# FFN of a diffusion step: weight parts and additions regrouped at the start of the up columns, prompt taps moved behind the sample taps, the last tile's product in two column halves

## Chip, core and metric

One core of one Trainium2 chip. The metric is the device time of one execution in microseconds (us); the kernel before took 1524.4 us (median of 3 runs, 1524.12 to 1524.8).

## What is computed

One layer of a diffusion backbone: a mixer of gated linear attention, then a feed-forward block with a convolution, for 128 prompt tokens and 1024 sample tokens (a grid of 16 rows of 64) with 1024 features. The change lies in the feed-forward block and the final norm:

```python
def conv_ffn(h, w_up, conv_w, conv_b, w_down, grid):
    u = dw_conv(h @ w_up, conv_w, conv_b, grid)      # 3x3 on the grid; width 3 on the prompt
    gate, up = jnp.split(u, 2, axis=-1)
    return (jax.nn.silu(gate) * up) @ w_down
...
    x = x + gate2 * conv_ffn(h, w_ffn_up, ffn_conv, b_ffn_conv, w_ffn_down, grid)
...
y_prompt = rmsnorm(xp, final_norm)
y_sample = rmsnorm(xs, final_norm)
```

The hidden width is 2816, which is 22 columns of 128; w_up gives each column a gate half and an up half. Everything is float32.

## The kernel before

**Numbers in two parts.** Each float32 operand is split into a high part (ScalarE copies it into the multiplier's format: `wuh`, `t4h`) and a low part (the rest, by a subtraction in `split_lo`, line 69: `wul`, `t4l`), and each product is three matmuls: high by high, low by high, high by low. Low parts are made by VectorE (DVE) or GpSimd (POOL).

**Seven products for eight.** Each up column multiplies two halves of the tokens with a 2x2 arrangement of weight blocks (11, 12, 21, 22) by a Winograd form: seven products of sums of weight blocks (s1 to s4) and sums of tokens (t1 to t4). `up(c, p)` is product p of column c: twelve 128x512 matmuls (line 1772). F and S are the column's two accumulators in PSUM, of 1024 tokens each (gate half and up half); there are three such buffers, so a column's S takes the buffer of the F or S before it once the convolution has read it. ScalarE copies some partial products out (`cp`, `u2p`), and DVE adds them into F and S.

**The convolution.** `conv_rows` lets ScalarE write the bias and the middle tap and DVE add eight taps (line 1937) of about 960 columns; `conv_prompt` does bias (line 1950) and two short taps (line 1954) for the prompt. The Silu (line 2033), the product of the two halves on POOL (line 2035) and a DMA to memory (`scr_g`) follow.

**Order.** For column 0 the order on each engine is written out by hand: `run(engine, fn)` appends an operation behind the last one of that engine. From column 1 on the order is set at build time by a scheduler that estimates durations. Around the change: `first_sums` (line 1848) makes t4, the last token sum, on DVE and splits it (`t4h` on ACT, `t4l` on DVE); between the two halves it splits weight block s1 of column 1 (line 1859, its low part on DVE) and does two F additions (lines 1861 and 1862). Then ACT and POOL split the other pairs of column 1 (11/12, s2/s4, 21/22), by `second_pair`. Column 0's prompt taps stand among its F taps.

**Down products.** After the 22 columns eight products of 11 weight pairs with w_down follow (line 2244), four banks of 128 tokens by 512 features each. At this seam POOL makes low parts of the first pairs (`wul`, `wl`) beside the last columns' gate products. The last product ends with `first_tokens`: for each of its four token tiles an addition into y with the gate (lines 2203 and 2204), a square with its sum on ACT (line 2208), and `finish` (lines 2215 to 2223): two small DVE steps, a power of -1/2 on POOL, two scalings, and the DMA out.

Of the kernel before, what the change touches and what calls it, by code (L numbers as in the profile page):

```python
# [8 lines left out]
F32 = mybir.dt.float32  # L9
# [8 lines left out]
P = 128  # L18
# [31 lines left out]
def kernel(ctx: ExitStack, tc: tile.TileContext, ins, outs, stop=None):  # L50
# [1696 lines left out]
    def split_slots(c, names, eng, both=False):  # L1747
# [9 lines left out]
        first = nc.scalar.activation(hi, raw, AF.Copy)  # L1757
        last = split_lo(eng, lo, raw, hi)
        return (first, last) if both else last
# [84 lines left out]
    def second_pair(*names):  # L1844
        with tc.issue_after(ran["act"].ins):
            ran["act"], ran["pool"] = split_slots(1, names, nc.gpsimd, both=True)

    def first_sums():
# [10 lines left out]
        run("act", lambda: nc.scalar.activation(hi, raw, AF.Copy))  # L1859
# [155 lines left out]
    def prompt_columns(c):  # L2015
# [9 lines left out]
        conv_prompt(pp[:, 1 if up_first else 0, :], c, acc[c][0])  # L2025
        conv_prompt(pp[:, 0 if up_first else 1, :], 22 + c, acc[c][1])
# [17 lines left out]
    for c in range(NHID + 1):  # L2044
# [47 lines left out]
        if c == 0:  # L2092
            up(c, 3)
            up_prompt(c, 0)
        if c and n:
# [19 lines left out]
        if c == 0:  # L2115
            run("act", copy_pt)
            second_pair("11", "12")
            with tc.issue_after(ran["act"].ins):
# [19 lines left out]
        if c == 0:  # L2138
            second_weights()
        elif n:  # L2140
# [51 lines left out]
    def load_y(t):  # L2192
# [3 lines left out]
        sq[t] = smp.tile([P, 4], F32, name=f"sq{t}", tag=f"sq{t}")  # L2196
# [3 lines left out]
    def add_gated(t, half, src, op=ALU.add):  # L2200

        e = ep.tile([P, 512], F32, name="e", tag="e")
        nc.vector.tensor_tensor(e, src, gate2[0 if t == 8 else 1][:, HF[half]], op=ALU.mult)
        nc.vector.tensor_tensor(ys[t][:, HF[half]], ys[t][:, HF[half]], e, op=op)

    def square(t, half):
        junk = ep.tile([P, 512], BF16, name="junk2", tag="junk2")
        nc.scalar.activation(junk, ys[t][:, HF[half]], AF.Square, accum_out=sq[t][:, half : half + 1])

    def finish(t, first):  # L2210

        y, q = ys[t], sq[t]
        last = 1 - first
        nc.vector.tensor_scalar(q[:, 2:3], q[:, first : first + 1], 1.0 / D, EPS, op0=ALU.mult, op1=ALU.add)
        nc.vector.scalar_tensor_tensor(  # L2215
            q[:, 2:3], q[:, last : last + 1], 1.0 / D, q[:, 2:3], op0=ALU.mult, op1=ALU.add
        )
        nc.gpsimd.tensor_tensor(q[:, 3:4], q[:, 2:3], mhalf[:, 0:1], op=ALU.pow)  # L2218
        nc.scalar.activation(y[:, HF[first]], y[:, HF[first]], AF.Copy, scale=q[:, 3:4])
# [3 lines left out]
        nc.sync.dma_start(y_prompt[0] if t == 8 else y_sample[0, t * P : (t + 1) * P, :], y)  # L2223

# [7 lines left out]
    def product(banks, start, stop, done, tail=0, head=0, beside={}):  # L2232

        for js in ([tuple(range(head))] if head else []) + [(j,) for j in range(head, NPAIR - tail)] + ([tuple(range(NPAIR - tail, NPAIR))] if tail else []):
# [4 lines left out]
            for i in range(4):  # L2239
                ts_ = slice(i * P, (i + 1) * P)  # L2240
                for j, w in zip(js, ws):
                    for n, (a, b) in enumerate(((0, 0), (0, 1), (1, 0))):
                        with tc.issue_after(anchor["down"].ins) if j < head else nullcontext():
# [139 lines left out]
```

## Time and profile before

| what | us |
|---|---|
| median of 3 runs | 1524.4 |
| profiled execution, whole | 1526.4 |
| its span in the trace | 1524.6 |
| PE busy (12494 matmuls) | 1470.2 (96%) |
| DVE busy | 1146.5 (75%) |
| ACT busy | 779.9 (51%) |
| POOL busy | 707.7 (46%) |
| mean granted TensorE clock | 0.992 |

PE is TensorE, PEld its weight loads, DVE VectorE, ACT ScalarE, POOL GpSimd, SP SyncE (which issues DMAs). Times in the trace count from the start of the span. PE's share is an average: to see what one edit can do, one reads what PE waits for in that stretch, since a wait of another engine matters only where PE comes to wait for it in turn. In a row of the trace `t4l<-acc,t4h` is the tile written and the tiles read, and L69 the line of the program.

### The profile page before, as it was taken

What the parts mean: (1) busy time and instruction counts of PE and PEld (TensorE: products, weight loads), DVE (VectorE), ACT (ScalarE), POOL (GpSimd) and SP (SyncE); (2) the same over time, 40 slices, a digit from 0 to 9 for tenths busy, and PEclk for the clock granted to TensorE, in tenths of its full rate; (3) what the DMA queues carried; (4) which work ended last, traced back from release to release, by engine and by line L of the source; (5) the groups of instructions that cost most, each with busy time, mean ns of one, the idle gap of its engine ahead of it and who ended that gap; (6) DMA issues with size and microseconds to landing.
All of it is one profiled execution on the core that took longest, in us unless ns stands there. A gap on an engine that the chain in (4) does not pass through costs nothing.

```text
span 1524.6 us, 31105 instructions
## 1 busy us (share of the span) xinstructions
PE 1470.2 (96%) x12494; PEld 1250.5 (82%) x12494; DVE 1146.5 (75%) x1731; ACT 779.9 (51%) x1517; POOL 707.7 (46%) x538
## 2 busy tenths in 40 slices
PE   6999999999999999899989999999999999999997
PEld 2798989999898998777777888888888877888886
DVE  3766566664565767656689999999999999689475
ACT  3575667555454555513664444454444444466444
POOL 1512123234233241223237999999999995100001
PEclk9999999999999999999999999999999999999999
DMA  9311111335435463777642564545644567979752
GB/s 335 136 43 48 47 54 52 121 93 191 139 108 173 126 204 119 273 275 258 221 146 78 179 191 113 148 116 143 193 116 139 171 159 229 352 257 371 238 189 115
DMA packets 173802, 253.79 MB, mean 166 GB/s; under 512 B 11828, under 2 KB 113698, under 8 KB 171738
## 3 DMA queue, kind: packets, MB, share of 16 engines
q1 hardware_dynamic: 150455, 173.52, 35.5%
q0 software_dynamic: 22592, 77.60, 16.4%
q8 instruction: 98, 1.61, 0.5%
q10 hardware_dynamic: 611, 0.68, 0.1%
q14 instruction: 46, 0.38, 0.1%
HBM read 191.93 MB, written 82.90 MB: 180 GB/s over the span
## 4 chain that ended last, share of the span: by engine, by line
PE 81%; DVE 5%; DMA 5%; ACT 3%; issue 3%; POOL 2%; SPq 0%; POOLq 0%; ACTq 0%; DVEq 0%
PE u L1772 26%; PE mm L625 15%; PE xb L2244 7%; PE yb L2244 6%; PE mm L639 5%; PE x L2003 4%; PE mm L775 3%; PE lv L962 3%; PE yb L2296 2%; PE u L1542 2%; PE mm L519 1%; PE x L1030 1%; DVE acc L1937 1%; DMA mh<-scr_m 1%; DMA wa<-in_w_ada_dram 1%
## 5 line engine op out<-in xcount | busy, mean ns | idle before, releaser
L1937 DVE SCALAR_TENSOR_TENSOR acc<-u,convc,acc 128x945 f32<-128x945 f32 (+2 forms) x352 | 426.8, 1218 | 7.3 <-ACT acc L1925 0.2
L69 POOL TENSOR_TENSOR wl<-raw,wh 128x1024 fp32r<-128x1024 f32 x42 | 102.4, 2444 | 249.8 <-ACT wh L133 195.5
L625 PE MATMUL mm<-h1h,wh 128*128 128x384 f32 x528 | 185.0, 350 | 0.6 <-ACT qj L528 0.6
L625 PE MATMUL mm<-h1h,wl 128*128 128x384 f32 x528 | 179.0, 339 | 0.0
L625 PE MATMUL mm<-h1l,wh 128*128 128x384 f32 x528 | 179.0, 339 | 0.0
L925 DVE TENSOR_TENSOR Q<-Q,fb 128x384 f32<-128x384 f32 x126 | 83.8, 665 | 87.8 <-PE lv L962 86.9
L69 POOL TENSOR_TENSOR wul<-sr,wuh 128x512 fp32r<-128x512 f32 (+1 forms) x64 | 119.6, 1868 | 16.5 <-ACT wuh L1757 16.4
L69 POOL TENSOR_TENSOR wul<-ra,wuh 128x1024 fp32r<-128x1024 f32 x44 | 115.2, 2617 | 19.1 <-ACT wuh L1757 19.1
L915 ACT ACTIVATE m<-k 128x384 f32<-128x384 f32 x126 | 70.2, 557 | 81.9 <-PE lv L962 39.4
L2218 POOL TENSOR_TENSOR sq<-sq,mhalf 128x1 f32<-128x1 f32 x9 | 11.1, 1232 | 205.1 <-DVE sq L2215 205.1
L625 PEld LDWEIGHTS mm<-h1h,wh 128*128 128x128 f32 x528 | 99.5, 188 | 5.5 <-issue 3.9
L625 PEld LDWEIGHTS mm<-h1l,wh 128*128 128x128 f32 x528 | 99.5, 188 | 0.6 <-issue 0.2
L625 PEld LDWEIGHTS mm<-h1h,wl 128*128 128x128 f32 x528 | 99.3, 188 | 0.8 <-issue 0.5
L639 PE MATMUL mm<-wh,h1h 128*128 128x256 f32 x288 | 84.5, 293 | 0.6 <-ACT v L664 0.5
L927 DVE TENSOR_TENSOR k<-k,fb 128x384 f32<-128x384 f32 x126 | 74.2, 589 | 10.7 <-ACT m L915 6.2
L639 PE MATMUL mm<-wh,h1l 128*128 128x256 f32 x288 | 81.2, 282 | 0.0
L639 PE MATMUL mm<-wl,h1h 128*128 128x256 f32 x288 | 81.2, 282 | 0.0
L133 ACT ACTIVATE wh<-raw 128x1024 fp32r<-128x1024 f32 x50 | 52.8, 1058 | 42.2 <-PE mm L625 11.4
L2035 POOL TENSOR_TENSOR acc<-acc,acc 128x1152 f32<-128x1152 f32 x22 | 61.1, 2779 | 15.1 <-DVE acc L1937 15.1
L1965 ACT ACTIVATE u2p<-u 128x512 f32<-128x512 f32 x44 | 26.5, 602 | 77.8 <-PE u L1772 77.8
L1757 ACT ACTIVATE wuh<-ra 128x1024 fp32r<-128x1024 f32 x42 | 44.3, 1054 | 34.5 <-issue 18.4
L639 PEld LDWEIGHTS mm<-wh,h1h 128*128 128x128 f32 x288 | 55.1, 191 | 3.4 <-issue 1.7
(386 smaller groups left out, 4470.0 us busy)
## 6 DMA issues: line engine op xcount, KB each, us to landing
ra<-in_w_ffn_up_dram SPq DMA_DIRECT2D x84, 256.0 KB, 3.3
raw<-in_w_in_dram SPq DMA_DIRECT2D x32, 512.0 KB, 4.7
v<-in_w_ada_dram SPq DMA_DIRECT2D x27, 512.0 KB, 4.7
scr_g<-acc POOLq DMA_DIRECT2D x22, 576.0 KB, 5.7
scr_s<-late POOLq DMA_DIRECT2D x11, 1024.0 KB, 5.4
scr_t<-in_w_ffn_down_dram POOLq DMA_DIRECT2D x16, 704.0 KB, 7.3
wa<-in_w_ada_dram SPq DMA_DIRECT2D x16, 512.0 KB, 5.7
scr_t<-in_w_ffn_down_dram POOLq DMA_DIRECT2D x2, 2816.0 KB, 12.7
```

The lines of the kernel that those rows point to most:

```text
L69: return eng.tensor_tensor(out, full, hi.bitcast(F32), op=ALU.subtract)
L133: nc.scalar.activation(hi, raw, AF.Copy)
L625: anchor["fill"] = mm(ps, a[:, kt, :], h[kt][b], start=(n == 0), stop=(n == 23))
L639: anchor["fill"] = mm(ps, h[kt][t // 3][:, ts_], a[:, kt % 4, :], start=(n == 0), stop=(n == 23))
L915: nc.scalar.activation(aps(t, 0, [[2 * h, NB], [h, 2], [1, h]]), aps(src, 0, [[2 * h, NB], [BL + h, 2], [1, h]]), AF.Copy)
L925: nc.vector.tensor_tensor(qm, qm, aps(ff_, 2 * h - 1, [[BL - h, 2], [2 * h, NB], [0, h]]), op=ALU.mult)
L927: nc.vector.tensor_tensor(km, km, aps(ff_, BL + 2 * h - 1, [[-(BL + h), 2], [2 * h, NB], [0, h]]), op=ALU.mult)
L1772: last = mm(dst, w_slot(c, a, x)[:, kt, :], HB[y][b][:, kt, :], start=(start and n == 0), stop=(stop and n == 11), skip_group_check=True,)
L1937: last = nc.vector.scalar_tensor_tensor(o, u3[:, r0 + dy : r1 + dy, c0 + dx : c1 + dx], wc(3 * (dy + 1) + dx + 1), o, op0=ALU.mult, op1=AL ...
L2003: last = mm(pk, HB[h]["p"][:, 4 * half + kt, :], aps(flat(W[x]), a * 512 + kt * P, [[(b - a) * 512, 2], [1, P]]), start=(half + kt + n == ...
L2035: last = nc.gpsimd.tensor_tensor(accg, accg, accu, op=ALU.mult)
L2244: anchor["down"] = mm(banks[i], w[a][:, ts_], w[b][:, 512:1024], start=(start and j == 0 and n == 0), stop=(j == NPAIR - 1 and n == 2), sk ...
```

## The change

Three regroupings:

1. Weight block s1 of column 1 is split earlier: its high part on ACT ahead of t4h, its low part on DVE ahead of the token sums. The high part of 11/12 follows s1's on ACT, and its low part moves from POOL to DVE, behind the F additions. The t4 split on DVE goes ahead of the two F additions. `second_pair` becomes `second_hi` and `second_lo`; the pairs s2/s4 and 21/22 are split at the head of column 1's turn in the loop.
2. For columns 0 and 1 the prompt's bias and taps are issued behind the F taps (`after("conv")`).
3. In the last product the last bank is multiplied in two halves of 256 columns, all five tail pairs for the one half and then for the other; its addition and its square go by halves too, with one more small sum, and tile 2's last scaling and DMA go behind the second half's addition.

```diff
+    def second_hi(*names):
+        hi, second[names] = split_parts(1, names)
+        run("act", hi)
+    def second_lo(*names, eng="pool"):
+        run(eng, lambda: second[names](nc.vector if eng == "dve" else nc.gpsimd))
...
         half_hi("t4", 0, tmp[2])
-        slot = SLOT[1]["s1"]
-        hi, lo = (flat(W[x][:, slot]) for x in "hl")
-        raw = flat(at(1, "s1"))
-        run("act", lambda: nc.scalar.activation(hi, raw, AF.Copy))
-        run("dve", lambda: split_lo(nc.vector, lo, raw, hi))
-        run("dve", lambda: tt(F[:, 0:512], F[:, 0:512], copies["p1"], op=ALU.add))
-        run("dve", lambda: tt(F[:, 512:NS], F[:, 512:NS], copies["u2"], op=ALU.add))
         half_hi("t4", 1, tmp[3])
         for n in range(2):
             half_lo("t4", n, tmp[2 + n])
+        run("dve", lambda: tt(F[:, 0:512], F[:, 0:512], copies["p1"], op=ALU.add))
+        run("dve", lambda: tt(F[:, 512:NS], F[:, 512:NS], copies["u2"], op=ALU.add))
+        second_lo("11", "12", eng="dve")
...
-        conv_prompt(pp[:, 1 if up_first else 0, :], c, acc[c][0])
-        conv_prompt(pp[:, 0 if up_first else 1, :], 22 + c, acc[c][1])
+        with after("conv") if c < 2 else nullcontext():
+            conv_prompt(pp[:, 1 if up_first else 0, :], c, acc[c][0])
+            conv_prompt(pp[:, 0 if up_first else 1, :], 22 + c, acc[c][1])
...
+        if c == 1:
+            for names in (("s2", "s4"), ("21", "22")):
+                second_hi(*names)
+                second_lo(*names)
+            second_weights()
...
         if c == 0:
             up(c, 3)
             up_prompt(c, 0)
+            second_hi("s1")
+            second_lo("s1", eng="dve")
+            second_hi("11", "12")
...
-            second_pair("11", "12")
-            with tc.issue_after(ran["act"].ins):
+            with tc.issue_after(ran["act"].ins), tc.issue_after(ran["dve"].ins):
                 anchor["conv"] = conv_rows(F, c, acc[c][0])
             ran["act"] = anchor["rows"]
-            second_pair("s2", "s4")
-            second_pair("21", "22")
...
+                cols = pieces if last and i == 3 and js[-1] == NPAIR - 1 else (slice(0, 512),)
+                for cs in cols:
+                    for j, w in zip(js, ws):
...
+                                    banks[i][:, cs],
+                                    w[a][:, ts_],
+                                    w[b][:, 512 + cs.start : 512 + cs.stop],
...
+                    if len(cols) > 1:
+                        last(i, cs)
...
+    def last_piece(i, cs):
+        fs = slice(512 + cs.start, 512 + cs.stop)
+        added = add_gated(i, 1, yb[i][:, cs], cs=fs)
+        square(i, 1, cs=fs, to=1 if cs.start == 0 else 4)
+        if cs.start:
+            with tc.issue_after(added.ins):
+                finish_rest(i - 1, 0)
+            finish_root(i, 0, parts=(1, 4))
+            finish_rest(i, 0)
```

`finish` is cut into `finish_root` (the small sums, the power, and the scaling on ACT) and `finish_rest` (the scaling on DVE and the DMA).

What this does to the order on an engine is seen at three places. The first is DVE around the t4 split, before; 9783 and 10298 are the two halves of the token sum, cp and u2p the copies that the F additions (L1861, L1862) read, and 9782 is the tile of F's convolution.

```order
L1407 TENSOR_TENSOR acc_10298<-rb_9794,acc_10298 128x1024
L1854 TENSOR_TENSOR u<-u,u2p_10302 128x512
L69 TENSOR_TENSOR wul<-sr,wuh 128x512
L1861 TENSOR_TENSOR u<-u,cp_10251 128x512
L1862 TENSOR_TENSOR u<-u,u2p_10302 128x512
L69 TENSOR_TENSOR t4l<-acc_9783,t4h 128x4x256
L69 TENSOR_TENSOR t4l<-acc_10298,t4h 128x4x256
L1937 SCALAR_TENSOR_TENSOR acc_9782<-u,convc,acc_9782 128x15x63
```

And the same stretch of DVE after the change (L1867 and L1868 are the F additions, L1941 is a tap).

```order
L69 TENSOR_TENSOR wul<-sr,wuh 128x512
L1407 TENSOR_TENSOR acc_9783<-rb_9794,acc_9783 128x1024
L1407 TENSOR_TENSOR acc_10298<-rb_9794,acc_10298 128x1024
L1862 TENSOR_TENSOR u<-u,u2p_10302 128x512
L69 TENSOR_TENSOR t4l<-acc_9783,t4h 128x4x256
L69 TENSOR_TENSOR t4l<-acc_10298,t4h 128x4x256
L1867 TENSOR_TENSOR u<-u,cp_10251 128x512
L1868 TENSOR_TENSOR u<-u,u2p_10302 128x512
L69 TENSOR_TENSOR wul<-ra,wuh 128x2x512
L1941 SCALAR_TENSOR_TENSOR acc_9782<-u,convc,acc_9782 128x15x63
```

The s1 low part went ahead of the sums, t4l ahead of the two F additions, and the 11/12 low part (`wul<-ra`) came over from POOL.

The second place is POOL at the seam from the columns to the down products, before: L2035 is column 20's gate product (acc3), `scr_g20` its DMA, and `wul` and `wl` are low parts of the first down pairs.

```order
L2035 TENSOR_TENSOR acc3_10298<-acc3_10298,acc2_9783 128x1152
L1910 DMA scr_t3_157<-in_w_ffn_down_dram 32x11x512
L69 TENSOR_TENSOR wul_10293<-ra_10290,wuh_10292 128x1024
L69 TENSOR_TENSOR wul_10293<-sr_10291,wuh_10292 128x1024
L2036 DMA scr_g20_139<-acc3_10298 128x1152
L1892 TENSOR_TENSOR late_10471<-acc3_10298 128x512
L69 TENSOR_TENSOR wl0_14091<-raw0_14096,wh0_14090 128x1024
L69 TENSOR_TENSOR wl1_14093<-raw1_14097,wh1_14092 128x1024
L69 TENSOR_TENSOR wul_10293<-sr_10291,wuh_10292 128x1024
```

POOL at the same place after the change.

```order
L69 TENSOR_TENSOR wul_10293<-ra_10290,wuh_10292 128x1024
L2040 TENSOR_TENSOR acc3_10298<-acc3_10298,acc2_9783 128x1152
L1914 DMA scr_t3_157<-in_w_ffn_down_dram 32x11x512
L69 TENSOR_TENSOR wul_10293<-sr_10291,wuh_10292 128x1024
L69 TENSOR_TENSOR wl0_14091<-raw0_14096,wh0_14090 128x1024
L69 TENSOR_TENSOR wl1_14093<-raw1_14097,wh1_14092 128x1024
L2041 DMA scr_g20_139<-acc3_10298 128x1152
L1896 TENSOR_TENSOR late_10473<-acc3_10298 128x512
L69 TENSOR_TENSOR wul_10293<-sr_10291,wuh_10292 128x1024
```

The first low part (`wul<-ra`) now stands ahead of the gate product, and the two `wl` ahead of its DMA and of the token difference `late`.

The third place is PE in the last bank after the change, where the first column half ends and the second begins (wuh and wul, wh2 and wl2 are parts of the tail pairs; a wait is in brackets).

```order
L2264 MATMUL yb_15203<-wh2_14094,wl2_14095 128x256
L2264 MATMUL yb_15203<-wuh_10292 128x256
L2264 MATMUL yb_15203<-wul_10293,wuh_10292 128x256
L2264 MATMUL yb_15203<-wuh_10292,wul_10293 128x256
L2264 MATMUL yb_15203<-wuh_10292 128x256 [waits DVE_49]
```

Before, the bank had 15 matmuls of 128x512 and no wait; now it has 30 of 128x256, and the sixteenth waits for DVE, which reads the first half of the same bank.

More of the change, by code (lines that the diff above doesn't have):

```diff
@@ L1756, in split_slots @@
             raw = raw.rearrange("p (s n) -> p s n", s=2)
-        first = nc.scalar.activation(hi, raw, AF.Copy)
-        last = split_lo(eng, lo, raw, hi)
-        return (first, last) if both else last
+        return lambda: nc.scalar.activation(hi, raw, AF.Copy), lambda eng: split_lo(eng, lo, raw, hi)
+    def split_slots(c, names, eng):
+        hi, lo = split_parts(c, names)
+        hi()
+        return lo(eng)
     def weight_sums(c, eng):
@@ L2223, in finish @@
         nc.sync.dma_start(y_prompt[0] if t == 8 else y_sample[0, t * P : (t + 1) * P, :], y)
+    def finish(t, first):
+        finish_root(t, first)
+        finish_rest(t, first)
     def times_norm(t, half):
@@ L2230, in load_norm, with product @@
             nc.sync.dma_start(fn, ins["final_norm"].rearrange("(o d) -> o d", o=1).to_broadcast([P, D]))
-    def product(banks, start, stop, done, tail=0, head=0, beside={}):
+    def product(banks, start, stop, done, tail=0, head=0, beside={}, last=None):
         for js in ([tuple(range(head))] if head else []) + [(j,) for j in range(head, NPAIR - tail)] + ([tuple(range(NPAIR - tail, NPAIR))] if tail else []):
@@ L2319, in first_tokens @@
         square(i, 1)
-        finish(i, 0)
-    product(yb, False, True, first_tokens, tail=5)
+        finish_root(i, 0)
+        if i < 2:
+            finish_rest(i, 0)
[7 more added lines that the diff above has]
+            finish_root(i, 0, parts=(1, 4))
+            finish_rest(i, 0)
+    product(yb, False, True, first_tokens, tail=5, last=last_piece)
 _INS = [
```

64 lines of the change are left out of this document (30 added, 34 removed).

## The prediction

> **What bounds the kernel now.** I read the waits of PE first, from the first up column to the end.
>
> ```profile
> PE u L1772 <- DVE acc L1937: 3.4, 2, 2.6
> PE u L1772 <- DVE t4l L69: 2.7, 1, 2.7
> PE u L1772 <- ACT wuh L1859: 1.0, 1, 1.0
> PE xb L2244 <- POOL wul L69: 0.9, 1, 0.9
> PE u L1772 <- ACT cp L1965: 0.8, 1, 0.8
> ```
>
> After the columns are total us, count, longest. Some 9 us in 744 are all that PE loses to others here; everything else it works. The windows say the same, and show what a wait drags behind it (per stretch: length, PE, PEld, DVE, ACT, POOL busy, granted clock, DMA share, GB/s).
>
> ```profile
> 795.00:800.00 5.00, 5.00 (x16) 3.94 (x16) 4.87 (x6) 1.18 (x2) 5.00 (x3) 0.66 0.16 47
> 800.00:820.00 20.00, 17.79 (x88) 14.22 (x87) 17.60 (x18) 9.90 (x14) 11.75 (x9) 1.00 0.14 40
> 820.00:1250.00 430.00, 430.00 (x2105) 356.10 (x2104) 417.95 (x442) 200.01 (x268) 418.09 (x277) 1.00 0.53 150
> ...
> 1255.00:1260.00 5.00, 2.99 (x7) 2.42 (x8) 4.93 (x6) 1.17 (x1) 4.02 (x4) 0.69 0.97 308
> ```
>
> From 820 to 1250 PE is busy 430.00 of 430.00 us at full clock, so nothing that the change shuffles inside those columns can pay, and what is gained or lost before 820 is carried on unchanged. In the first and last row the clock falls to 0.66 and 0.69, each at a long wait. The chain of waits (start, length, what) gives the steps.
>
> ```profile
> 790.31 4.44 DVE t4l L69 x2
> ...
> 794.79 9.85 PE u L1772 x35
> 804.64 2.84 PE x L2003 x24
> ...
> 1285.14 21.83 PE xb L2244 x95
> 1306.97 29.92 PE yb L2244 x132
> ```
>
> A 128x512 product steps by 29.92/132 = 0.227 us, a 128x256 one by 2.84/24 = 0.118. Behind 1285.14 each piece of PE begins where the last one ends (1285.14 + 21.83 = 1306.97, and so on to the last product), so a delay there reaches the end whole. Three places can therefore move the time: the start of the columns (787 to 820), the seam to the down products (1267 to 1285), and the tail behind the last product.
>
> **First part, the start of the columns.** Two kinds of work are drawn forward and one is taken away.
>
> ```profile
> 780.67 2.35 DVE L69 TENSOR_TENSOR t3l<-acc,t3h 128x1024 fp32r<-128x1024 f32 x2
> ...
> 786.66 1.06 ACT L1410 ACTIVATE t4h<-acc 128x1024 fp32r<-128x1024 f32 x1 [5.38 <-DVE acc L1407]
> ...
> 788.27 0.69 DVE L69 TENSOR_TENSOR wul<-sr,wuh 128x512 fp32r<-128x512 f32 x1 [1.03 <-ACT wuh L1859]
> ...
> 790.21 4.52 DVE L69 TENSOR_TENSOR t4l<-acc,t4h 128x1024 fp32r<-128x1024 f32 x2
> 794.66 2.44 DVE L1937 SCALAR_TENSOR_TENSOR acc<-u,convc,acc 128x945 f32<-128x945 f32 x2
> ...
> 790.48 3.17 POOL L69 TENSOR_TENSOR wul<-ra,wuh 128x1024 fp32r<-128x1024 f32 x1 [19.11 <-ACT wuh L1757]
> ```
>
> Rows here and below are of the timeline: start, length, engine, line, and in brackets the idle time ahead and what ended it. ACT is idle 5.38 us ahead of t4h, and there the s1 hi part now goes: PE's 1.00 us wait disappears, and the s1 lo part (0.69, of which DVE steps 0.61) stands ahead of the token sums, which end near 787.2 instead of 786.6. Then the two t4l follow at once, with POOL not working: 2.35 as t3l's pair takes, not 4.52 beside POOL's 3.17. They end at 790.7; PE, 1.2 us earlier, waits some 0.5 for them instead of 2.7. The two F additions (0.69 each) and the 11/12 lo part, now DVE's (half of 2.35), come behind: F0's taps start at 793.3, 1.35 ahead of 794.66.
>
> Now what is late next. With no prompt taps among them the eight F0 taps (2.44/2 = 1.22 each, a little more where one needs the last) end near 803.3. S0's eight taps, four short prompt taps (0.3 each, an estimate: with 127 columns each is less than half an addition of 512) and three additions (0.69) are 13 us of DVE, with its short waits for the copies: 816.5. PE meanwhile is done with its independent work, which in the chain ends at 804.64 + 2.84 = 807.5, some 5.5 us earlier (waits of 1.0 and 2.2, and 1.7 of the slow clock behind 795), stands from 802 to 803.4 for F0's buffer (gap 1.5), ends up(1,1) at 806.2, and waits for the cp copy. That copy stands on ACT behind the Silu with its table load:
>
> ```profile
> 807.97 1.28 ACT L2033 ACT_TABLE_LOAD   x1
> 809.26 1.17 ACT L2033 ACTIVATE acc<-acc 128x1152 f32<-128x1152 f32 x1
> 810.34 0.58 ACT L1965 ACTIVATE cp<-u 128x512 f32<-128x512 f32 x1
> ...
> 818.46 0.47 PE L1772 MATMUL u<-t1h,wuh 128*128 128x512 f32 x1 [0.77 <-DVE acc L1937]
> ```
>
> The Silu needs the prompt taps, last at 804.8 now; 1.28, 1.17 and 0.58 from 805.3 give 808.1, a gap of 2.0 on PE instead of 0.8. Then 12 products, the u2 copy, 12 more to 814.5, and a wait for S0's last tap: the first product of column 2 starts at 816.6 instead of 818.46, **1.85 us earlier**, out of the 4 us that PE is ahead at 795. The rest has become three gaps of 1.5, 2.0 and 2.1.
>
> Gaps have a price. The windows at 0.66 and 0.69 hold the waits of 2.7 and 2.6; at 0.66, 0.34 of 5.00 us are missing, 1.7 us, which is 3.4 us at half clock, and PE pays it wherever it works through the whole of it. The Trainium skill ("TensorE: Matmul & The Clock Gate", Part 1: The HAM clock gate) has the half rate return only after an idle window of some 3.4 us; by that rule none of the new gaps costs anything, and the start is worth the full 1.85. This trace disagrees: 2.6 and 2.7 were enough.
>
> Waits of 0.8 drew none: the clock from 800 to 820, where the cp wait lies, is 1.00. Between 1.0 and 2.6 I have no row in these parts; 2.0 and 2.1 are nearer to 2.6, so I take a slow stretch after both. The first lengthens up(1,6) and by it the copy, S0's taps and the start of column 2 by 1.2; the second costs about 1.0, as PE stands through part of it. Term: -1.85 + 1.2 + 1.0 = **+0.35 us**; ends -1.85 (no stretch) and +1.5 (both paid in full, or one behind the 1.5 gap as well).
>
> **Second part, the seam.** Nobody edits it, but POOL's order there changes: pair 2's lo part (wul<-ra) now stands ahead of column 20's gate product.
>
> ```profile
> 1267.62 2.69 POOL L2035 TENSOR_TENSOR acc<-acc,acc 128x1152 f32<-128x1152 f32 x1 [7.46 <-DVE acc L1937]
> 1270.26 1.10 POOL L1910 DMA_DIRECT2D scr_t<-in_w_ffn_down_dram  x1
> 1270.98 2.83 POOL L69 TENSOR_TENSOR wul<-ra,wuh 128x1024 fp32r<-128x1024 f32 x1
> 1273.64 2.53 POOL L69 TENSOR_TENSOR wul<-sr,wuh 128x1024 fp32r<-128x1024 f32 x1
> 1275.98 0.73 POOL L2036 DMA_DIRECT2D scr_g<-acc  x1
> 1276.61 1.42 POOL L1892 TENSOR_TENSOR late<-acc 128x512 f32<-128x512 f32 x1
> 1277.87 4.86 POOL L69 TENSOR_TENSOR wl<-raw,wh 128x1024 fp32r<-128x1024 f32 x2
> 1282.60 2.49 POOL L69 TENSOR_TENSOR wul<-sr,wuh 128x1024 fp32r<-128x1024 f32 x1
> ...
> 1268.50 1.05 ACT L133 ACTIVATE wuh<-ra 128x1024 fp32r<-128x1024 f32 x1
> ...
> 1268.63 2.75 DVE L69 TENSOR_TENSOR wl<-ra,wh 128x1024 fp32r<-128x1024 f32 x1 [0.25 <-ACT wh L133]
> ...
> 1275.32 0.48 PE L2244 MATMUL xb<-wuh 128*128 128x512 f32 x1
> ```
>
> POOL has no idle time from 1267.62 to 1285.09, where pair 4's lo part releases PE. All eight instructions remain, in another order, so the end shifts as the start does. The queue's head now waits for ACT's hi part (1268.50 + 1.05 = 1269.55), and then beside DVE's wl (itself behind one more addition and S20's last tap, so near 1269.4 to 1270.6, at 1.2 without the product beside it). Two such operations at once took 2.75 and 2.83 instead of 1.2 and 2.4, one held up by the other; so POOL's first gets going at 1270.65, 3.03 later than 1267.62, and takes 0.26 less than its old step of 2.66. Pair 4 comes at 1285.09 + 3.03 - 0.26 = 1287.9, **+2.75 us**. On the way pair 3's lo part (needed by the eighth product from 1275.32, at 1277.0) comes at 1278.85, a gap of 1.9; pair 4's is then another of 2.0. A slow stretch after the first is hidden in the second. Ends: +1.7 where POOL starts at 1269.6 unhindered, +4.4 where the second gap draws a stretch of 1.7.
>
> **Third part, the tail.**
>
> ```profile
> 1516.02 0.39 PE L2244 MATMUL yb<-wuh,wul 128*128 128x512 f32 x1
> ...
> 1516.45 0.69 DVE L2203 TENSOR_TENSOR e<-yb,gate 128x512 f32<-128x512 f32 x1 [0.44 <-PE yb L2244]
> ...
> 1518.49 0.63 ACT L2208 ACTIVATE junk<-y 128x512 bf16<-128x512 f32 x1 [1.10 <-DVE y L2204]
> ...
> 1519.49 0.55 POOL L2218 TENSOR_TENSOR sq<-sq,mhalf 128x1 f32<-128x1 f32 x1 [2.85 <-DVE sq L2215]
> ...
> 1520.07 0.75 DVE L2220 SCALAR_TENSOR_TENSOR y<-y,sq,fn 128x512 f32<-128x512 f32 x1 [0.67 <-POOL sq L2218]
> ```
>
> From the last product's end (1516.41) to the last scaling's (1520.82) lie 4.41 us, with tile 2's scaling between the two additions. The second column half needs a multiplication and an addition of 128x256 (0.43 each, an estimate: 0.69 at 512 and 1.18 at 1024 give it by a straight line), a square (between 0.3 and 0.63; I take 0.4, and 0.2 until its sum is there, since 1518.49 + 0.63 is 0.4 ahead of the POOL row), then 0.16, 0.55 and 0.75 and hand-overs of 0.03 to 0.09: 3.2, so 1.2 less. Against it: 30 products of 0.118 are 0.14 longer than 15 of 0.227, and PE's first product of the second half waits for DVE's multiplication of the first (they share a bank): a product's end 0.3 after its start (0.39 at 512), the multiplication 0.43 behind tile 2's addition, hand-overs, together 0.75 beyond a step. Term: -1.2 + 0.14 + 0.75 = **-0.3 us**; ends -1.2 (wait gone) and +0.2 (128x256 as dear as 512).
>
> **Sum.** +0.35 + 2.75 - 0.3 = +2.8 us. Against the profiled execution's 1526.4 that is 1529.2; that execution lay 2.0 above the median of the runs, so for the median 1524.4 + 2.8 = **1527.2**. It is 0.18%, and 0.2% (3.05 us, about what a measurement of this kernel can tell from no change) is just not reached.
>
> **Rivals.**
> 1. Slower: half clock behind pair 4's gap. If the 1.9 gap for pair 3 draws no stretch and the 2.0 gap does, 1.7 is added whole, PE having no wait behind it. For it speaks 0.69 after 2.6; against it that the first gap is just as long. It decides from a gap somewhere between 1.0 and 2.6. 1527.2 + 1.7 = 1528.9.
> 2. No stretch after gaps of about 2 at the columns' start: 1524.4 - 1.85 + 2.75 - 0.3 = 1525.0. For it: the page's rule, and no row of a 2.0 gap there. Against: two of two long ones did.
> 3. The seam's order is harmless, POOL's chain having slack that the rows hide: 1524.4 + 0.35 - 0.3 = 1524.4 or, with rival 2, 1522.2. Against it stands that POOL has no idle time there and PE's one wait ends on it.
> 4. All goes well: rivals 2 and 3, PE's 0.9 wait gone too and the tail's wait absent: -1.85 - 0.9 - 1.2 = -3.95, 1520.4.
>
> **How the numbers follow.** Forecast 0.42; rivals 0.26, 0.15, 0.10, 0.07. The forecast's own spread (0.8 either way from where the slow stretches fall) puts 0.10 of its 0.42 beyond 3.05. Slower: 0.26 + 0.10 = 0.36; same: 0.32 + 0.15 + 0.10 = 0.57; faster: 0.07. The range leaves out rival 4, the deep end of 3, and the cases with more than one extra stretch: 1522.6 to 1529.6.
>
> **What would show it.** Right: t4l as two of 1.2 us and no PE wait for the s1 part; PE waits near 803, 806 and 814 of 1.6, 2.0 and 2.1 us, with a clock well below 1.00 behind them; two waits on POOL's wul of about 1.9 instead of one of 0.9; one PE wait on DVE's e of about 0.8 in the last bank. Wrong: one wait or none on POOL at the seam, or a clock of 1.00 from 806 to 825; then the sum is 2 to 3 us too high. Columns 2 to 19 with PE waits would break the step on which everything is carried.

## The result, and the profile after

The changed kernel takes 1527.47 us (median) against 1524.12 for the kernel before in the same runs: ratio **1.0031 [1.002, 1.0041]**, 0.31% or some 4.7 us slower, more than the 0.2% that a measurement can tell. By the two medians alone it is 3.35 us, 0.22%. One of its eleven runs took 2064 us at a granted clock of 0.65, and the ratio leaves it out. The profiled execution took 1530.77 us, with a span of 1528.8.

The waits of PE from the first up column to the end, after (total us, count, longest):

```profile
PE u L1775 <- DVE acc L1941: 3.8, 2, 2.6
PE xb L2264 <- POOL wul L69: 3.5, 2, 1.9
PE u L1775 <- ACT cp L1969: 2.1, 1, 2.1
PE u L1775 <- ACT wuh L1757: 2.0, 1, 2.0
PE u L1775 <- ACT u2p L1969: 0.7, 1, 0.7
PE yb L2264 <- DVE e L2213: 0.6, 1, 0.6
```

Against before, the wait for s1's high part (1.0) is gone and the one for t4l is down from 2.7 to 0.3. New or longer are the cp wait (0.8 before), a 2.0 us wait ahead of column 2, a second wait for POOL's low parts, and the one in the tail. The windows (length, PE, PEld, DVE, ACT, POOL busy, granted clock, DMA share, GB/s):

```profile
805.00:810.00 5.00, 2.94 (x11) 2.09 (x10) 4.26 (x6) 3.19 (x4) 3.92 (x4) 0.89 0.00 0
810.00:815.00 5.00, 4.31 (x14) 3.13 (x13) 2.85 (x4) 2.09 (x4) 0.90 (x1) 0.77 0.01 3
815.00:820.00 5.00, 3.02 (x12) 2.15 (x12) 4.91 (x6) 3.48 (x4) 5.00 (x3) 0.91 0.18 52
820.00:825.00 5.00, 5.00 (x19) 3.97 (x18) 4.86 (x5) 0.95 (x2) 5.00 (x4) 0.74 0.44 129
830.00:1250.00 420.00, 419.87 (x2059) 348.02 (x2058) 405.94 (x428) 195.69 (x262) 405.07 (x269) 1.00 0.53 150
```

From 800 to 820 the clock had been 1.00 before; now two half-clock stretches lie behind two waits of 2 us (0.89 with 0.77, and 0.91 with 0.74). From 830 to 1250 PE works 419.87 of 420.00 us, so what is lost ahead of it is carried to the end. Column start, after, PE's rows with a wait (start, length, ..., idle time ahead and what ended it):

```profile
803.20 0.50 PE L1775 MATMUL u<-b11h,wuh 128*128 128x512 f32 x1 [1.13 <-DVE acc L1941]
808.27 0.50 PE L1775 MATMUL u<-t2h,wuh 128*128 128x512 f32 x1 [2.06 <-ACT cp L1969]
813.56 0.50 PE L1775 MATMUL u<-t3h,wuh 128*128 128x512 f32 x1 [0.69 <-ACT u2p L1969]
818.56 0.47 PE L1775 MATMUL u<-t1h,wuh 128*128 128x512 f32 x1 [1.99 <-ACT wuh L1757]
```

The last row names a copy on ACT. In the program that product waits for this copy and for DVE's last S0 tap. The copy had long been made; what ended just ahead of the product is the tap, the first of the nine in the last row of DVE here:

```profile
788.07 2.36 DVE L69 TENSOR_TENSOR t4l<-acc,t4h 128x1024 fp32r<-128x1024 f32 x2 [0.52 <-ACT t4h L1410]
...
807.18 0.34 DVE L1958 SCALAR_TENSOR_TENSOR acc<-x,convc,acc 128x127 f32<-128x127 f32 x1
808.25 0.70 DVE L2119 TENSOR_TENSOR u<-u,cp 128x512 f32<-128x512 f32 x1 [0.73 <-ACT cp L1969]
...
813.54 0.70 DVE L2120 TENSOR_TENSOR u<-u,u2p 128x512 f32<-128x512 f32 x1 [2.12 <-ACT u2p L1969]
...
816.61 0.70 DVE L2145 TENSOR_TENSOR u<-u,u2p 128x512 f32<-128x512 f32 x1
817.22 11.13 DVE L1941 SCALAR_TENSOR_TENSOR acc<-u,convc,acc 128x945 f32<-128x945 f32 x9
```

The two t4l take 1.2 us each, as forecast. Later DVE stands idle for 2.12 us, waiting for a copy of what PE computes at half clock, and takes an S addition (L2145) ahead of that last tap. At ACT one sees why the cp copy is late:

```profile
804.80 0.46 ACT L1954 ACTIVATE acc<-x,vcol,convc 128x128 f32<-128x128 f32 x1 [2.25 <-DVE acc L1958]
805.28 1.28 ACT L2038 ACT_TABLE_LOAD   x1
806.57 1.16 ACT L2038 ACTIVATE acc<-acc 128x1152 f32<-128x1152 f32 x1
807.64 0.58 ACT L1969 ACTIVATE cp<-u 128x512 f32<-128x512 f32 x1
```

The prompt's bias on ACT waits 2.25 us for a prompt tap on DVE; table load, Silu and cp copy stand behind it in ACT's queue.

The seam, after: DVE's order, then POOL's.

```profile
1269.35 0.70 DVE L2120 TENSOR_TENSOR u<-u,u2p 128x512 f32<-128x512 f32 x1 [0.23 <-ACT u2p L1969]
1269.96 1.19 DVE L1941 SCALAR_TENSOR_TENSOR acc<-u,convc,acc 128x945 f32<-128x945 f32 x1
```

```profile
1271.30 3.26 POOL L69 TENSOR_TENSOR wul<-ra,wuh 128x1024 fp32r<-128x1024 f32 x1 [9.56 <-ACT wuh L133]
1274.52 2.70 POOL L2040 TENSOR_TENSOR acc<-acc,acc 128x1152 f32<-128x1152 f32 x1
...
1286.78 2.77 POOL L69 TENSOR_TENSOR wul<-sr,wuh 128x1024 fp32r<-128x1024 f32 x1
```

POOL starts its chain at 1271.30 instead of 1267.62, and ends it at 1289.55 instead of 1285.09; PE waits for its low parts 1.86 and 1.67 us where it had waited 0.89. On DVE column 20's last tap now stands behind column 21's second F addition. The tail:

```profile
1519.85 0.39 PE L2264 MATMUL yb<-wuh 128*128 128x256 f32 x1 [0.59 <-DVE e L2213]
```

**Where the time went.** To compare executions I count from the first product of column 0 with token sum t3 (at 782.26 before, 782.03 after), and put places in the program beside each other:

| us from there | before | after | difference | predicted |
|---|---|---|---|---|
| first product of column 2 | 36.20 | 36.53 | +0.33 | |
| first product of column 3 | 58.69 | 60.40 | +1.71 | |
| first down product | 493.06 | 494.96 | +1.90 | +0.35 |
| seam, to the second down product | 31.49 | 34.28 | +2.79 | +2.75 |
| from there to PE's end | 209.60 | 210.63 | +1.03 | +0.9 |
| PE's end to the last scaling | 4.41 | 3.13 | -1.28 | -1.2 |
| sum | 738.56 | 743.00 | +4.44 | +2.8 |

Seam and tail came as reckoned; the column start cost 1.55 us more in this execution. That row differs from one execution to the next: e1_seam, e7_dveseam and e10_both below leave the column start as it is in the kernel after. With the same two waits on PE (2.06 to 2.08 and 1.98 to 1.99), column 3 starts there at 58.92, 57.31 and 60.48, with one, no and two half-clock stretches. Why the seam moved at all was open.

### The profile page after: what moved, and what is told of

It is laid out like the page before. It is cut to its first block, busy times and chain, and to the rows that moved or that the text cites. A ratio compares the mean times of both kernels' runs of the same rounds, so it can differ in the third digit from the quotient of the medians.

```text
span 1528.8 us, 31137 instructions
## 1 busy us (share of the span) xinstructions
PE 1471.1 (96%) x12509; PEld 1252.9 (82%) x12509; DVE 1142.4 (75%) x1735; ACT 780.3 (51%) x1519; POOL 704.4 (46%) x537
## 4 chain that ended last, share of the span: by engine, by line
PE 78%; DMA 6%; DVE 4%; ACT 4%; issue 4%; POOL 3%; SPq 0%; POOLq 0%; DVEq 0%; ACTq 0%
PE u L1775 23%; PE mm L625 15%; PE xb L2264 7%; PE yb L2264 6%; PE mm L639 5%; PE x L2007 3%; PE mm L775 3%; PE lv L962 3%; PE yb L2318 2%; PE u L1542 2%; PE x L1030 1%; PE mm L519 1%; DMA raw<-in_w_in_dram 1%; DMA mh<-scr_m 1%; DVE acc L1941 1%
## 5 line engine op out<-in xcount | busy, mean ns | idle before, releaser
L1941 DVE SCALAR_TENSOR_TENSOR acc<-u,convc,acc 128x945 f32<-128x945 f32 (+2 forms) x352 | 426.9, 1218 | 7.4 <-ACT acc L1929 0.2
L925 DVE TENSOR_TENSOR Q<-Q,fb 128x384 f32<-128x384 f32 x126 | 80.4, 638 | 89.2 <-PE lv L962 88.5
L69 POOL TENSOR_TENSOR wul<-ra,wuh 128x1024 fp32r<-128x1024 f32 x43 | 111.4, 2591 | 9.6 <-ACT wuh L133 9.6
L1757 ACT ACTIVATE wuh<-sr 128x512 fp32r<-128x512 f32 (+1 forms) x63 | 48.7, 772 | 23.1 <-PE x L2007 17.3
```

The lines of the kernel that those rows point to most:

```text
L69: return eng.tensor_tensor(out, full, hi.bitcast(F32), op=ALU.subtract)
L925: nc.vector.tensor_tensor(qm, qm, aps(ff_, 2 * h - 1, [[BL - h, 2], [2 * h, NB], [0, h]]), op=ALU.mult)
L1757: return lambda: nc.scalar.activation(hi, raw, AF.Copy), lambda eng: split_lo(eng, lo, raw, hi)
L1941: last = nc.vector.scalar_tensor_tensor(o, u3[:, r0 + dy : r1 + dy, c0 + dx : c1 + dx], wc(3 * (dy + 1) + dx + 1), o, op0=ALU.mult, op1=AL ...
```

## The experiments

The ratio is always to the kernel before, run beside each kernel. "Column 3" and "seam" are the positions and lengths of the table, from one profiled execution each.

**e1_seam: POOL's seam order as before.**

```diff
-        return load_w([a, b], [2 * 512], nc.gpsimd if p == 1 and j < 6 else nc.vector)
+        with after("gate20") if p == 1 and j > 0 else nullcontext():
+            return load_w([a, b], [2 * 512], nc.gpsimd if p == 1 and j < 6 else nc.vector)
...
+        if c == NHID - 2:
+            anchor["gate20"] = last
```

> The changed kernel with one thing put back: at the seam POOL's low part of pair 2 and those behind it stand behind column 20's gate product again, as before; every other engine's order is that of the change. Theory (POOL's order costs 2.9 us at the seam): PE's two waits on wul of 1.86 and 1.67 us become one of about 0.9, and the time falls by 2.9 from the change's 1527.5 to about 1524.6. Rival (the seam is late because the columns, the DMAs or DVE are late): the two waits stay near 1.8 and the time at 1527.5.

Measured: 1.0023 [1.0011, 1.0035], seam 34.28, waits 1.35 and 1.68. The seam was not repaired: POOL's product now heads the queue, but starts at 1265.80 in this execution (3.54 us long), just behind DVE's last S20 tap (1264.45 + 1.19). My theory that POOL's order alone does it fell.

**e7_dveseam: DVE's seam order as before**, POOL's as in the kernel after.

```diff
-            nc.vector.tensor_tensor(F[:, 512:NS], F[:, 512:NS], copies["u2"], op=ALU.add)
+            with after("up") if last_c else nullcontext():
+                nc.vector.tensor_tensor(F[:, 512:NS], F[:, 512:NS], copies["u2"], op=ALU.add)
```

> The changed kernel with one thing put back on DVE: column 21's second F addition, which waits for a copy, stands behind column 20's last tap again, as before; POOL keeps the order of the change. e1_seam, with POOL's order alone, left both waits on wul (1.35 and 1.68). Theory now (DVE's order makes the gate product late, POOL's order is the scheduler's answer to it; each alone delays pair 4): about 0.9 to 1.1 less than the change, since POOL's first low part still waits for ACT's high part: waits of about 1.3 and 1.6, 1526.4. Rival (DVE's order alone is the cause): 2.9 less, one wait of 0.9.

Measured: 1.003 [1.0017, 1.0042], seam 34.28 again (waits 1.87 and 1.23): neither the 0.9 to 1.1 us of the theory nor the 2.9 of the rival. Either order alone is enough to lose 2.8 us.

**e10_both: both edits.**

> The changed kernel with both put back at the seam: DVE's order of e7_dveseam and POOL's of e1_seam. Theory (the two together are the whole loss at the seam): one wait on wul of 0.9 to 1.1 us, the stretch from the first xb product to the first yb product as in the kernel before (31.5 us, against 34.3 in the change), 2.8 less than the change. Rival (something else at the seam is late, such as a DMA): it stays over 33.

Measured: 1.0024 [1.0013, 1.0035], seam 32.39: 1.9 of the 2.8 us are back. The two POOL waits are gone, and a wait that they had hidden comes out, at the third accumulator of the down products:

```profile
1280.87 0.47 PE L2268 MATMUL xb<-wuh 128*128 128x512 f32 x1 [2.05 <-DVE acc L1959]
```

L1959 is a prompt tap: this accumulator takes over the PSUM bank that column 21's prompt taps read. In the kernel before, the same wait stands at the fourth accumulator, nine products later, where it is over.

**e2_cpfirst: e1_seam with the cp copy ahead of the Silu on ACT.** `gate_half` holds column 0's Silu, its product and DMA.

```diff
             up(c, 1)
+            if c == 1:
+                with after("copy"):
+                    gate_half(0)
```

> The kernel of e1_seam, and on ACT the cp copy of column 1 stands ahead of column 0's Silu and its table load. Theory (a wait of 2.06 us on PE draws a stretch of half clock that costs up(1,6) another 1.65 us): PE's wait for cp falls to about 0.8, no slow stretch follows it, column 2's first product comes about 3.1 us earlier than in the change; time about 3 below e1_seam, near 1521.5. Rival (the clock is not set by that wait): only the 1.3 us of the shorter wait are gained, time 1.3 below e1_seam, and the clock behind 808 still falls.

Measured: 1.0014 [1.0005, 1.0023], below e1_seam by 2.2 us in the medians and 1.4 in the ratios, whose intervals overlap; the theory had 3, the rival 1.3. The cp wait is 0.69 and column 3 starts at 57.52 (e1_seam 58.92). No half-clock stretch lies behind that wait, but none lay behind the 2.08 of e1_seam's profiled execution either: the 1.4 us between the positions are the shorter wait alone, and this pair does not show what a stretch costs.

**e4_warm: e1_seam with six useless products on PE** in the cp wait, into a buffer that is overwritten later.

```diff
+            if c == 1:
+                for i in range(6):
+                    chained(lambda: mm(u[1][1][:, 512:NS], w_slot(1, "11", "h")[:, 0, :], HB["h"]["b11"][:, 0, :], start=True, stop=True, skip_group_check=True))
```

> The kernel of e1_seam, and PE does six useless 128x512 products (into a part of PSUM that is overwritten later) behind up(1,1), while it would wait for the cp copy, which comes as late as in the change. Theory (idle time on PE itself lowers the clock): the wait shrinks from 2.06 to about 0.7, up(1,6) starts no earlier but runs at full clock, and column 2 starts 1.65 us earlier; time 1.65 below e1_seam, near 1523. Rival (lateness of the data is what costs, not the clock): no gain, or a loss of a few tenths.

Measured: 1.0005 [0.9996, 1.0013], column 3 at 57.78. up(1,6) ran at full clock, as it had in e1_seam's profiled execution. But the scheduler also moved DVE's last S0 tap ahead of the S addition, and at the seam it put DVE's last taps and POOL's low parts back in the order of the kernel before: the seam is 32.34, with the third accumulator's wait (2.04) and none for POOL, as in e10_both. Of the 2.05 us by which the positions lie below e1_seam's, 1.94 come from the seam, so this run does not test the clock. A new wait of 1.93 at column 3 drew a stretch in its turn.

**e8_lasttap: the S addition behind the previous column's last tap**, up to column 20, and the F taps of columns 1 to 3 behind that tap too.

```diff
-            nc.vector.tensor_tensor(S[:, 512:NS], S[:, 0:512], copies["p5"], op=ALU.add)
+            with after("up") if not last_c else nullcontext():
+                nc.vector.tensor_tensor(S[:, 512:NS], S[:, 0:512], copies["p5"], op=ALU.add)
...
-            anchor["conv"] = conv_rows(F, c, acc[c][0])
+            with after("up") if c < 4 else nullcontext():
+                anchor["conv"] = conv_rows(F, c, acc[c][0])
```

> The changed kernel, and on DVE the S additions of columns 1 to 20 stand behind the last tap of the column before, as they did for column 1 in the kernel before; the first F taps of columns 2 and 3 are held behind those too. In the change the last S0 tap, which frees the buffer for column 2, stands behind an addition that waits for up(1,7), so that PE always waits 1.99 there. Theory: that wait falls to about 1.3, and no slow stretch follows it; column 3 starts 2.3 us earlier than in the change, about 2.3 less. Rival (1.3 us idle draws the stretch just as well): 0.65 less.

Measured: 1.0019 [1.001, 1.0028], column 3 at 59.23 (after 60.40): 1.2 us earlier, where the theory had 2.3 and the rival 0.65. The wait ahead of column 2 falls from 1.99 to 1.38 and draws no stretch; 0.94 us come back as a wait ahead of column 3.

**e6_tail: the kernel before with the tail part of the change alone** (the hunks on the last product and its sums, part 3).

> The kernel before with the change's third part alone (last bank in two column halves). Theory: PE waits 0.6 to 0.8 us for DVE's multiplication between the halves, the finish behind the last product is 1.2 us shorter, so 0.3 us less in all, within what can be told: 1523.8. Rivals: the wait is as long as the gain (0), or the halves gain the full 1.2 (1522.9).

Measured: 0.9994 [0.9986, 1.0003]; PE's wait 0.59, tail 3.13, as in the kernel after. Time and positions (-0.25) agree within the interval.

**e9_best: e10_both, e8_lasttap and the cp copy first, together.**

> e10_both, e8_lasttap and the cp copy ahead of the Silu (e2_cpfirst) in one kernel. Theory: PE waits of 1.2, 0.7, 0.7 and about 1.3 at the start of the columns and no slow stretch, one wait of 1 us at the seam, 0.6 in the tail: column 3 starts 3.2 earlier than in the kernel before, the seam costs nothing more, the tail gives 0.3, in all 3.5 below the kernel before, a ratio of 0.9977. Rival (the parts overlap, since DVE is as late as PE): 1 to 2 below the kernel before.

Measured: 1.0001 [0.9992, 1.0011], not the 0.9977 of the theory; column 3 at 56.38, seam 32.36 with the third accumulator's wait (2.1). By positions it lies 2.0 us below the kernel before, by the runs it does not.

**e11_banks: e9_best with the third and fourth accumulator in each other's bank.**

```diff
-    ps_b, ps_c = (ps_d[1], ps_d[3]), (ps_d[0], ps_d[2])
+    ps_b, ps_c = (ps_d[1], ps_d[1], ps_d[4], ps_d[3]), (ps_d[0], ps_d[0], ps_d[2], ps_d[2])
```

> This is e9_best with the third and the fourth accumulator of the down products put into each other's PSUM bank, so that the one written third lies where column 21's ACT copy, not its prompt taps, was read last. Theory (the seam's last 0.9 us are a wait of 2.05 us for that bank): the wait moves to the fourth accumulator, nine products (2 us) later, where it is over; the seam goes from 32.36 to 31.5 us, as in the kernel before, no PE wait of 1 us or more between the last gate product and the first yb product; the time is 0.9 us below e9_best's 1522.9, so 1522.0. Rival (the wait is on the prompt taps wherever the accumulators lie, or pair 4's lo part is the next to be late): seam 32.2 to 32.4, time as e9_best's.

Measured: 1.0 [0.9991, 1.0008]. The bank's wait is gone and the seam 31.76, with pair 4's wait left, as in the kernel before:

```profile
1283.12 0.49 PE L2278 MATMUL xb<-wul,wuh 128*128 128x512 f32 x1 [1.10 <-POOL wul L69]
```

**e12_taps: e11_banks with column 0's prompt taps free.**

```diff
-        with after("conv") if c < 2 else nullcontext():
+        with after("conv") if c == 1 else nullcontext():
```

> This is e11_banks with column 0's four prompt taps no longer held behind its token taps (column 1's stay held). Theory (VectorE has no idle time from 788 to 825 here, so that the place of four taps of 0.34 us among its 26 us of work moves what PE waits for but not when VectorE is through): the last F0 tap comes up to 1.4 us later, the PE wait ahead of up(1,1) grows by that and the waits behind it shrink by as much; the start of column 3 stays within 0.5 us of e11_banks', and so does the time. Rival (the order that the change sets is worth what it holds back): 1.0 to 1.4 us slower than e11_banks. A gap of over 2 us that draws a half-clock stretch would add up to 1.7 to either.

Measured: 1.0 [0.999, 1.001], column 3 at 55.94. The held order is worth nothing here. And the seam is 32.36 again, with a 2.1 us wait for a prompt tap at the third accumulator: freeing four taps of column 0 has put the prompt columns, up to column 21, in the other bank, so that the exchange now harms. The guard reaches the seam.

**e14_free: the kernel after without the guard on the prompt taps, all else as in the change.**

```diff
-        with after("conv") if c < 2 else nullcontext():
-            conv_prompt(pp[:, 1 if up_first else 0, :], c, acc[c][0])
-            conv_prompt(pp[:, 0 if up_first else 1, :], 22 + c, acc[c][1])
+        conv_prompt(pp[:, 1 if up_first else 0, :], c, acc[c][0])
+        conv_prompt(pp[:, 0 if up_first else 1, :], 22 + c, acc[c][1])
```

> This is the kernel after with the one guard left out that holds the prompt taps of columns 0 and 1 behind the token taps; all else of the change stands. In its program order VectorE and GpSimd stand at column 20 and 21 as in the kernel before (column 20's last tap ahead of column 21's second F addition, column 20's gate product ahead of pair 2's lo part), and the prompt columns lie in the other one of their two PSUM banks. Theory (the guard, at columns 0 and 1, is what shifts the seam 480 us later, through the order in which buffers come free): the seam is 31.5 us as before, one POOL wait of 0.9, no wait of 2 us for the third bank; the tail as after (PE wait 0.6, 3.13). At the column start the last F0 tap comes 1.36 us later (PE wait 1.1 + 1.4 = 2.5, with a half-clock stretch behind it in some executions), the cp wait falls from 2.06 to about 0.7, and column 3 starts 0 to 2 us earlier than the after kernel's 60.40. Time 2.8 to 4.8 us below the after kernel's ratio of 1.0031: ratio 1.000 to 1.0013. Rival (the seam's loss comes from the weight parts regrouped ahead of it, not from the guard): seam 34.28, ratio 1.002 to 1.003.

Measured: 1520.05 us, **0.9984 [0.9975, 0.9993]**: 7 us below the kernel after by the ratios (0.47%), and below the kernel before, by less than 0.2% but with an interval that leaves out 1. Column 3 starts at 56.01, the seam is 31.54, the sum 735.64 against 738.56 before and 743.00 after. The waits of PE:

```profile
PE u L1775 <- DVE acc L1941: 5.5, 4, 2.6
PE xb L2263 <- POOL wul L69: 0.9, 1, 0.9
PE u L1775 <- ACT u2p L1969: 0.7, 1, 0.7
PE u L1775 <- ACT cp L1969: 0.7, 1, 0.7
```

The cp wait is 0.7 and the seam has its one wait of 0.9 back. Column start, PE and then ACT:

```profile
798.57 0.50 PE L1775 MATMUL u<-b11h,wuh 128*128 128x512 f32 x1 [1.48 <-DVE acc L1941]
802.27 0.50 PE L1775 MATMUL u<-t2h,wuh 128*128 128x512 f32 x1 [0.69 <-ACT cp L1969]
805.97 0.50 PE L1775 MATMUL u<-t3h,wuh 128*128 128x512 f32 x1 [0.69 <-ACT u2p L1969]
809.53 0.47 PE L1775 MATMUL u<-t1h,wuh 128*128 128x512 f32 x1 [0.55 <-DVE acc L1941]
```

```profile
791.08 0.45 ACT L1954 ACTIVATE acc<-x,vcol,convc 128x128 f32<-128x128 f32 x1
...
798.59 1.28 ACT L2037 ACT_TABLE_LOAD   x1 [1.02 <-DVE acc L1941]
799.88 1.17 ACT L2037 ACTIVATE acc<-acc 128x1152 f32<-128x1152 f32 x1
801.62 0.60 ACT L1969 ACTIVATE cp<-u 128x512 f32<-128x512 f32 x1 [0.56 <-PE u L1775]
```

The bias runs at 791 (its row in the kernel after: 804.80, with 5 us between the two executions' clocks), the Silu waits for the last F tap alone, and the copy waits for PE's product, so that PE waits for the copy itself alone (0.69). With the taps among them the F taps end only 0.35 us later (a wait of 1.48 for 1.13; I had expected 2.5). The clock behind these waits (columns as above):

```profile
800.00:805.00 5.00, 4.31 (x19) 3.14 (x18) 4.93 (x5) 1.66 (x2) 3.96 (x4) 1.00 0.01 2
805.00:810.00 5.00, 3.76 (x16) 2.63 (x15) 4.92 (x6) 4.68 (x6) 3.48 (x2) 1.00 0.01 2
810.00:815.00 5.00, 5.00 (x25) 4.09 (x24) 3.88 (x5) 1.85 (x4) 5.00 (x3) 1.00 0.38 108
```

And the seam's head, DVE and POOL, in the order of the kernel before (the last S20 tap is the second of the two at 1257.04, ahead of the F addition):

```profile
1257.04 2.45 DVE L1941 SCALAR_TENSOR_TENSOR acc<-u,convc,acc 128x960 f32<-128x960 f32 x2
1259.71 0.70 DVE L2119 TENSOR_TENSOR u<-u,u2p 128x512 f32<-128x512 f32 x1 [0.23 <-ACT u2p L1969]
```

```profile
1259.64 2.69 POOL L2039 TENSOR_TENSOR acc<-acc,acc 128x1152 f32<-128x1152 f32 x1 [7.52 <-DVE acc L1941]
```

Between the kernel after and this one PE's program order is the same throughout. POOL's differs in some fifty places over all the columns, DVE's in columns 0 and 1 and then at columns 20 and 21, ACT's in columns 0 and 1. The rival, that the regrouped weight parts alone move the seam, falls. The guard alone on the kernel before was not run; its program has DVE and POOL at the seam in the order of the kernel after, and the prompt columns in that kernel's bank.

**e13_all: e12_taps with the banks as before.**

> This is e12_taps with the accumulators' banks as in the kernel before (not exchanged). Since the free prompt taps of column 0 put the prompt columns in the other bank, the exchange of e11_banks is now what harms. Theory: the wait of 2.1 us at the third accumulator goes, pair 4's lo part waits 1.1 us as in e11_banks; seam 31.5 to 31.8 instead of 32.36, column start as in e12_taps (column 3 at 55.9), sum 0.6 us below e12_taps' 735.92 in positions and in time: 1521.2 against 1521.8, ratio to before 0.998 to 1.000. Rival (the wait stays at the third accumulator): seam 32.36, time as e12_taps'.

Measured: 0.9986 [0.9978, 0.9995], seam 31.72, column 3 at 55.99, the third accumulator's wait gone. The repairs of e9_best on top of a free column 0 bring nothing beyond e14_free.

## Why the prediction was right, and where it was not

1. **The t4 split and the F taps**: right. t4l is two of 1.2 us, PE waits 0.3 for it, and the F0 taps end at 803.1 (predicted 803.3), the wait there 1.13 (1.5 to 1.6).
2. **The cp copy**: right in place and size (2.06 for 2.0; the prediction's own 1.28, 1.17 and 0.58 from 805.3 give 808.3, not 808.1), and for the reason given: it stands behind a Silu that needs the prompt taps, and behind a bias that waits for the same tap.
3. **Column start, +1.90 for +0.35: the failed step**, "The first lengthens up(1,6) and by it the copy, S0's taps and the start of column 2 by 1.2; the second costs about 1.0, as PE stands through part of it". up(1,6) takes 4.60 us (from 808.27 to 813.56 less the wait of 0.69) for e14_free's 3.01 at full clock: 1.6, not 1.2. PE stood through no part of the second stretch, so column 2 took 23.87 us instead of 22.49: 1.4, not 1.0. And the S addition ahead of the last S0 tap, counted only as work, holds the start of column 2: e8_lasttap takes 0.6 off that wait. These give 1.4 of the missing 1.55; the rest lies behind column 3 (1.90 less 1.71). The sum took both stretches as drawn. In this execution both came, and that is luck: behind the same two waits e7_dveseam drew neither, and its column 3 starts 1.4 us ahead of the kernel before's instead of 1.7 behind.
4. **The seam, +2.79 for +2.75**: right in size and in its waits (1.86 and 1.67 for 1.9 and 2.0). The mechanism was too narrow: POOL's order and DVE's each suffice, and a third wait for a PSUM bank, unseen in the prediction, lay hidden beneath both. No half-clock stretch followed the second wait (1.67), which was rival 1.
5. **What moved the seam.** The prediction took the order as given. It comes from part 2 of the change, the guard on the prompt taps of two columns 460 us earlier, as e14_free shows by leaving it out: 2.74 us at the seam and 4.63 at the column start, of 7.36 in all by positions (by the medians of the runs 5.7). The column start's share is worked out from waits that are 2.46 shorter (5.87 against 3.41), two stretches of 1.6 and 1.4 that are not drawn, and one new wait of 0.86 at column 2: 4.6. The two stretches are a draw of the kernel after's profile; without the guard no wait there is over 1.48, and none was drawn.
6. **The tail, -0.25 for -0.3**: right. From one half's last product (1518.98) to the other's first (1519.85) PE steps 0.87 us instead of 0.12, the 0.75 of the prediction; the end is 1.28 shorter.
7. **The sum** was 1.6 us short, all of it in step 3, and so "slower by over 0.2%" held where "within 0.2%" had the larger chance. The range held the time. That 1527.2 lies 0.3 from the median is in part luck, since the ratio says 4.7 us and the positions 4.4 where 2.8 was forecast. Rival 2 (no stretch after gaps of 2 us) is neither true nor false: see below. By the page of the Trainium skill that stands behind it ("TensorE: Matmul & The Clock Gate", Part 1) half rate returns only after an idle window of some 3.4 us; the rows here, where 2.06 and 1.99 us were enough, disagree.

What stays open: by which of its estimates the scheduler, with the guard in place, takes another order at column 20 was not traced. And single profiles are draws: by positions e11_banks is 2.6 us below before, by its runs 0.0% [-0.09, 0.08]. Before's profile holds two half-clock stretches from column 0 on (behind its waits of 2.75 and 2.64), e11_banks' none.

## What to carry to other kernels

Where a scheduler sets the order, an ordering hint on two early iterations can move queues hundreds of microseconds later: compare the whole program order of each edit by itself, and leave out one hint at a time before repairing the places where the loss shows. Work that is put last on one engine takes along what another engine has queued behind its result; here four taps of 0.3 us on DVE held a bias, a Silu and a copy on ACT, and by the copy PE. When a wait is removed, ask which wait ended just before it: restoring POOL's order alone or DVE's alone left the seam at 34.28, and only with both in place did the wait for the bank come out. And look at more than one execution: a row of one profile can hold a stretch that the next does not draw.

## What was not expected of the hardware

Whether a wait of about 2 us draws a half-clock stretch differs from one execution to the next. In the fourteen profiles the 2.64 us wait at column 20, the same in every kernel, drew one in seven and none in seven. Waits of 1.93 to 2.08 at the column start drew one 8 times in 11, the 2.7 us wait of the kernel before and of e6_tail both times. None of the seventeen waits of 1.0 to 1.5 there did, nor, at the seam, any of seven of 1.86 to 2.1.

What decides is where the wait falls. All seventeen stretches between column 0 and the last product are 3.41 us long, and within one execution their starts lie whole multiples of 3.41 us apart: the clock changes on a grid of 3.41 us, which lies elsewhere in each execution. These windows are cut on that grid (columns as above), in the kernel after and then in e7_dveseam, at the same two waits:

```profile
805.49:808.90 3.41, 1.35 (x7) 0.81 (x6) 2.67 (x6) 2.72 (x3) 3.33 (x3) 1.00 0.00 0
808.90:812.31 3.41, 3.41 (x10) 2.65 (x9) 2.49 (x3) 0.00 (x0) 0.10 (x1) 0.50 0.01 2
815.73:819.14 3.41, 1.43 (x7) 0.91 (x6) 3.39 (x4) 2.75 (x4) 3.41 (x2) 1.00 0.03 10
819.14:822.55 3.41, 3.41 (x10) 2.63 (x9) 3.30 (x4) 0.00 (x0) 3.41 (x3) 0.50 0.51 149
```

```profile
804.45:807.86 3.41, 1.73 (x7) 1.42 (x8) 2.67 (x4) 1.62 (x2) 1.93 (x2) 1.00 0.00 0
807.86:811.28 3.42, 2.73 (x12) 1.94 (x11) 2.81 (x4) 2.06 (x4) 0.87 (x1) 1.00 0.01 5
811.28:814.69 3.41, 1.60 (x8) 0.98 (x6) 3.36 (x5) 3.41 (x5) 3.41 (x3) 1.00 0.00 0
814.69:818.10 3.41, 3.23 (x15) 2.70 (x16) 3.34 (x4) 0.28 (x2) 3.41 (x2) 1.00 0.55 159
```

In the kernel after PE is idle for 2.06 and 1.98 us of a window (3.41 less its busy time), and the next window runs at 0.50. In e7_dveseam the grid cuts both waits, 1.68 and 1.81 us are the most that fall into one window, and the clock stays at 1.00. Over the fourteen traces, between column 0 and the last product, each of the 17 windows with 1.93 us or more of idle PE has a half-clock window behind it, and none of those with 1.88 or less has, 14 of them over 1.5. This bound is read off the traces; no run moved a wait on purpose, and in the mixer, ahead of these columns, a window with 1.54 drew one.

A stretch costs up to 1.7 us. So here a wait under 1.9 us costs its own length, and a longer one its own length plus a share of 1.6 us: if the grid may lie anywhere, a wait of 2.0 puts 1.9 into one window in about half of the executions, and one of 2.64 in two thirds (estimates from 1.9 and 3.41).
